# A fused diffusion step: VectorE's chain of Hyena's long convolution cut into finer steps between weight splits

## The chip, the cores and the metric

The kernel runs on one core of one Trainium2 chip. The metric is the device time of one execution in microseconds (us); a lower time is better. Before the change the median of three runs is 1741.65 us (1736.06 to 1744.64).

## The reference

The kernel computes one inference step of a two-layer backbone for 128 context tokens and 512 latent tokens (T = 640 together) with a model width of 1024. Layer 0 mixes by attention on one half of the channels and by Hyena, a long convolution, on the other half; layer 1 is a bidirectional mLSTM; each layer ends with a gated ConvFFN. Around each sub-layer stand an RMS norm and a shift, scale and gate worked out from the conditioning vector (`mod` below). What the change touches is Hyena in layer 0:

```python
def hyena_mixer(u, conv_w, conv_b, w1, b1, w2, b2, w3, b3, sin_freq, skip):
    L = u.shape[1]
    uc = dwconv3(u, conv_w, conv_b)
    x0, x1, v = uc[..., :HY_CH], uc[..., HY_CH:2 * HY_CH], uc[..., 2 * HY_CH:]
    v = (v * x1).astype(jnp.float32)
    h_f, h_b = hyena_filters(L, w1, b1, w2, b2, w3, b3, sin_freq)
    y = long_conv(v, h_f) + jnp.flip(long_conv(jnp.flip(v, axis=1), h_b), axis=1) + skip * v
    return (y * x0).astype(u.dtype)
...
out = jnp.concatenate([attn, hyo], axis=-1) @ w_out
```

`long_conv` is a convolution over the whole sequence by a Fourier transform; `u` is the Hyena part of the input projection `x @ w_in`, and `attn` is softmax attention with a norm and a rotary position (rope) on q and k.

## The kernel before, in words

**Matmuls.** Inputs are float32. A weight tile `wr` (128x1024, loaded by DMA through SyncE, SP) is split into two parts: ScalarE (ACT) casts `wh <- wr`, VectorE (DVE) subtracts `wl <- wr, wh`. TensorE (PE) then makes three products for each pair of tiles: `wh` with the high part of the activation, `wl` with the high part, `wh` with the low part. So no weight tile can be used by PE before ACT's cast and, behind it, DVE's subtraction. In the trace all engine calls stand at line 284 (a helper that records them), matmuls at line 365, transposes at line 376.

**Stages around the change.** The columns of the input projection of Hyena come in twelve tiles, named `u` in the trace, 48 matmuls each. When a tile is done, a width-3 convolution makes `zh` from it: one ACT instruction, then four on DVE. The eight tiles of x1 and v come first, then q, k and v (`qkv`), then the last four tiles, x0, whose `zh` is multiplied into the result of the long convolution by GpSimd (POOL), `vx<-zh,vx`. While PE works at `qkv` and at these last four tiles, DVE and ACT have the long convolution to do, in two halves of 256 channels (`long_conv`, lines 1312 on). Each half has transforms by matmul, sums of them (`forward`, lines 1112 on), products with the filter's spectrum for two groups, g0 and g1 (four products, two sums and four butterflies of halves each), four last sums (`vx`, `vz`), and inverse transforms by matmul (`iy`, `iz`). In the same stretch q and k of token tiles 0 to 4 are normed: ACT squares them, a chain of eleven small DVE instructions makes one over the root (`qn0` to `qn4`), ACT scales by it, DVE multiplies by the gains (`qkg`), POOL or DVE makes the rope products (`qrt`, `qru`), DVE adds them, PE transposes (`qkt`) and ACT copies the result (`qkT`). Then come attention (scores `s`, maximum `mx`, exponential `p`, transposes `pt`, result `po`), the output projection of layer 0 (`o`) in four groups of tokens, and the FFN. The gate that the output projection needs, mod(0,2), is summed on DVE from weights loaded by DMA: two `acc <- mw` instructions for each `mw` tile (`mw` has two buffers), at the end cast (`moda`), split (`modb`) and spread over the partitions by matmul (`modp`).

**What sets the order.** The program is written into each engine's queue in an order that a planner chooses while the kernel is built (class `Order`, lines 60 to 249). The matmuls are the main line. Everything else is a side task, a Python generator. A plain `yield` lets the task go on only when the results it has issued are planned to be done; `yield 0` lets it go on as soon as the planner's PE clock allows. At each call of `pump` (line 191) the planner first looks whether DVE and ACT are planned to be free within `FIRST` = 2500 ns of its clock. If they are, the next weight tile is split; only then do side tasks get a turn. Splits can so stand only between steps of a side task, never within one. The long convolution runs as one side task for both halves with a lead of `HLEAD` = 5000 ns, and has these places where a step can end:

```python
            nc.vector.tensor_tensor(o, x, y, op=op)
            if FINE and n % FINE == FINE - 1:
                yield 0
```

```python
            if FINE:
                yield 0
            nc.vector.tensor_tensor(x[0], x[0], x[1], op=ALU.subtract)
            nc.vector.tensor_tensor(C, C, S, op=ALU.add)
            if FINE:
                yield 0
```

With `FINE = 0` the eight sums of `forward` are one step, and so are the ten instructions of g0 and the ten of g1.

Of the kernel before, what the change touches and what calls it, by code (L numbers as in the profile page):

```python
# [325 lines left out]
def hybrid_step(ctx: ExitStack, tc: tile.TileContext, A: dict, O: dict):  # L326
# [785 lines left out]
    def forward(src, cols, out, name):  # L1112
# [24 lines left out]
        for n, (o, x, y, op) in enumerate(((out[0][:, a], c[:, a], c[:, b], ALU.add), (out[0][:, b], c[:, a], c[:, b], ALU.subtract),  # L1137
# [5 lines left out]
            nc.vector.tensor_tensor(o, x, y, op=op)  # L1143
            if FINE and n % FINE == FINE - 1:
                yield 0
        yield

    FINE = 0

    def filters():  # L1150
        z, w = hy["z"], hy["w"]
# [160 lines left out]
    def long_conv(hf):  # L1312
# [17 lines left out]
        HYE.tensor_tensor(vp[:, h1], vp[:, h1], gr, op=ALU.mult)  # L1330
        if FINE:
            yield 0
# [8 lines left out]
        for n in range(2):  # L1341
# [4 lines left out]
            HYE.tensor_tensor(S, S, gc, op=ALU.mult)  # L1346
# [6 lines that stand above are left out]
# [951 lines left out]
```

## Time and profile before

| | us |
|---|---|
| median of 3 runs (lowest, highest) | 1741.65 (1736.06, 1744.64) |
| the profiled execution, its own time | 1739.15 |
| its span, first to last instruction | 1737.3 |
| TensorE (PE) busy | 1683.4, 97% of the span |
| VectorE (DVE) busy | 1243.6, 72% |
| ScalarE (ACT) busy | 746.3, 43% |
| GpSimd (POOL) busy | 353.8, 20% |
| mean granted TensorE clock | 0.987 of full |

The span is that of the profiled execution; 1.85 us of its time lie around it. An engine's busy time is the time in which an instruction of it ran, waits not counted. A number in square brackets behind an instruction in the rows below is the time for which the engine had stood idle before it, with what ended the wait. A row "x4" of the timeline joins four instructions of one form in a row; its time is from the first one's start to the last one's end. The stretch of interest, from the last part of `qkv` to the start of the FFN of layer 0, lies between 229 and 385 us.

### The profile page before, as it was taken

To read this page: it belongs to the slowest core of one execution; us is meant where nothing else is said; L and a number is where in the kernel's file an instruction comes from. 1 tells how busy PE (TensorE), PEld (TensorE's weight loads), DVE (VectorE), ACT (ScalarE), POOL (GpSimd) and SP (SyncE) were. 2 spreads that over 40 slices of the span, in tenths; PEclk is the share of its full clock that TensorE was granted. 3 is DMA by queue.
4 is the path that set the end of the run, shared out by engine and by line. 5 is a ranking of instruction groups with operands and counts; after the bars stand their busy time and mean duration, and the time that the engine had idled before them with its cause. 6 is when DMAs were issued, how large, how long until landed. Compare 5 with 4: busy or idle time off the path is not lost. (4 is left out here: it accounts for less than half of the span.)

```text
span 1737.3 us, 25489 instructions
## 1 busy us (share of the span) xinstructions
PE 1683.4 (97%) x10074; PEld 1523.0 (88%) x10074; DVE 1243.6 (72%) x2057; ACT 746.3 (43%) x1233; POOL 353.8 (20%) x187
## 2 busy tenths in 40 slices
PE   7899899999999999999999999997999999999997
PEld 2778787789999999888899999996899999998886
DVE  4788797878878888797766888886578744445365
ACT  3422545545434344455565344334354423333343
POOL 0000121001546454340013111120015411111000
PEclk9999999999999999999999999998999999999999
DMA  9245132412434434454523212122124322223343
GB/s 359 91 152 170 37 101 101 169 38 99 158 121 143 144 119 154 153 198 129 188 89 137 70 47 83 57 69 100 49 77 147 125 77 74 73 74 109 132 159 122
DMA packets 64352, 203.85 MB, mean 117 GB/s; under 512 B 7335, under 2 KB 12455, under 8 KB 64234
## 3 DMA queue, kind: packets, MB, share of 16 engines
q1 hardware_dynamic: 64234, 202.23, 33.9%
q8 instruction: 79, 1.29, 0.3%
q14 instruction: 39, 0.32, 0.1%
HBM read 196.17 MB, written 3.94 MB: 115 GB/s over the span
## 5 line engine op out<-in xcount | busy, mean ns | idle before, releaser
L284 DVE TENSOR_TENSOR wl<-wr,wh 128x1024 fp32r<-128x1024 f32 (+1 forms) x260 | 317.9, 1228 | 107.8 <-ACT wh L284 107.6
L284 ACT CAST wh<-wr 128x1024 fp32r<-128x1024 f32 (+1 forms) x260 | 263.5, 1018 | 146.7 <-PE dn L365 104.1
L284 POOL TENSOR_TENSOR hid<-zg,zu 128x640 f32<-128x640 f32 x44 | 105.5, 2398 | 318.5 <-DVE zu L284 305.9
L284 DVE SCALAR_TENSOR_TENSOR acc<-mw,sc,acc 128x1024 f32<-128x1024 f32 x91 | 168.3, 1868 | 2.7 <-DMA mw<-in_w_mod 2.4
L284 POOL TENSOR_TENSOR acc<-acc,modp 128x1024 f32<-128x1024 f32 x49 | 146.2, 2984 | 115.4 <-ACT modp L284 91.2
L284 DVE SCALAR_TENSOR_TENSOR zg<-g,vec,zg 128x127 f32<-128x127 f32 (+3 forms) x168 | 87.4, 541 | 89.4 <-ACT zg L284 86.4
L365 PE MATMUL dn<-wh,hh 128*128 128x512 f32 x440 | 139.1, 396 | 1.8 <-DVE zu L284 1.6
L365 PE MATMUL dn<-wl,hh 128*128 128x512 f32 x440 | 138.2, 394 | 0.0
L365 PE MATMUL dn<-wh,hl 128*128 128x512 f32 x440 | 138.1, 394 | 0.0
L284 DVE SCALAR_TENSOR_TENSOR zu<-u,vec,zu 128x511 f32<-128x511 f32 (+2 forms) x164 | 86.7, 549 | 62.8 <-ACT zu L284 59.9
L284 ACT ACTIVATE zu<-u,vec 128x640 f32<-128x640 f32 (+1 forms) x42 | 36.8, 876 | 173.8 <-PE u L365 173.8
L365 PE MATMUL u<-a3h,wh 128*128 128x384 f32 (+1 forms) x336 | 104.7, 312 | 0.8 <-DVE a3h L284 0.8
L365 PE MATMUL g<-a3h,wh 128*128 128x384 f32 (+1 forms) x336 | 104.8, 312 | 0.0
L365 PE MATMUL g<-a1h,wh 128*128 128x384 f32 (+1 forms) x336 | 104.8, 312 | 0.0
L365 PE MATMUL u<-a3l,wh 128*128 128x384 f32 (+1 forms) x336 | 104.1, 310 | 0.5 <-POOL a3l L284 0.5
L365 PE MATMUL u<-a3h,wl 128*128 128x384 f32 (+1 forms) x336 | 104.3, 310 | 0.2 <-DVE wl L284 0.2
L365 PE MATMUL u<-a1h,wl 128*128 128x384 f32 (+1 forms) x336 | 104.2, 310 | 0.2 <-DVE wl L284 0.2
L365 PE MATMUL u<-a1h,wh 128*128 128x384 f32 (+1 forms) x336 | 104.2, 310 | 0.0
L365 PE MATMUL g<-a3h,wl 128*128 128x384 f32 (+1 forms) x336 | 104.1, 310 | 0.0
L365 PE MATMUL g<-a3l,wh 128*128 128x384 f32 (+1 forms) x336 | 104.1, 310 | 0.0
L365 PE MATMUL g<-a1h,wl 128*128 128x384 f32 (+1 forms) x336 | 104.0, 310 | 0.0
L365 PE MATMUL u<-a1l,wh 128*128 128x384 f32 (+1 forms) x336 | 104.0, 310 | 0.0
(742 smaller groups left out, 4452.2 us busy)
## 6 DMA issues: line engine op xcount, KB each, us to landing
wr<-in_w_up SPq DMA_DIRECT2D x92, 512.0 KB, 3.3
wr<-in_w_down SPq DMA_DIRECT2D x82, 512.0 KB, 3.3
mw<-in_w_mod SPq DMA_DIRECT2D x80, 512.0 KB, 4.4
wr<-in_w_ml SPq DMA_DIRECT2D x34, 512.0 KB, 3.6
wr<-in_w_out SPq DMA_DIRECT2D x18, 512.0 KB, 4.2
wr<-in_w_in SPq DMA_DIRECT2D x13, 512.0 KB
wr<-in_w_u SPq DMA_DIRECT2D x12, 512.0 KB, 5.2
we<-in_w_mod SPq DMA_DIRECT2D x8, 512.0 KB, 7.3
```

The source lines that it names most:

```text
L284: r = f(*args, **kw)
L365: r = nc.tensor.matmul(out, lhsT, rhs, start=start, stop=stop)
```

## The change

One number is changed, from 0 to 2:

```diff
@@ -1145,7 +1145,7 @@
                 yield 0
         yield
 
-    FINE = 0
+    FINE = 2
 
     def filters():
```

Now `forward` may be left after every second of its eight sums, and `long_conv` after the first four products, after the four products of g0 and of g1, and after the two sums behind each of these. No instruction is added or removed. What moves is the order in which the planner writes them: in the first half of the channels nothing but buffer numbers changes, in the second half and behind it, up to the start of the FFN of layer 0, the order changes on every engine; after that only one pair of `modp` matmuls in layer 1 stands one group of matmuls later.

VectorE, second half of the channels, from the end of `forward`: `vx` and `vf` are the tiles of the long convolution, `qsq` the q and k of token tile 2, `wl` a weight split, `qn3v` the first of the eleven of `qn3`.

```order
+L284 TENSOR_TENSOR vx_1773<-vf_1595,g0c 128x512
+L284 TENSOR_TENSOR vx_1774<-vf_1596,g0s 128x512
+L284 TENSOR_TENSOR vf_1595<-vf_1595,g0s 128x512
+L284 TENSOR_TENSOR vf_1596<-vf_1596,g0c 128x512
 L284 TENSOR_TENSOR qsq_1533<-qsq_1533,qrt_1691 128x6x64
 L284 TENSOR_TENSOR qsq_1533<-qsq_1533,qru_1692 128x6x64
-L284 TENSOR_TENSOR wl_1799<-wr_1699,wh_1798 128x1024
-L284 TENSOR_TENSOR wl_1811<-wr_1730,wh_1810 128x1024
-L284 TENSOR_SCALAR qn3v<-qss_1790 128x6
+L284 TENSOR_TENSOR vx_1773<-vx_1773,vx_1774 128x512
+L284 TENSOR_TENSOR vf_1595<-vf_1595,vf_1596 128x512
+L284 TENSOR_TENSOR wl_1811<-wr_1699,wh_1810 128x1024
```

The products and sums of g0 now stand ahead of the split and of `qn3`; one weight split (second of the last four `u` tiles) stands there instead of two (second and third). The third one's split moves behind `qn3` and a `zh`.

ScalarE around the cast of the fourth of these `u` tiles' weights, `wr_1757`. Before:

```order
L284 ACTIVATE qj_1952,qss_1951<-qsq_1816 128x128 x6
L284 ACTIVATE zh_2001<-u_1919,vec 128x640
L284 CAST wh_2014<-wr_1757 128x1024
L284 ACTIVATE zh_2064<-u_2007,vec 128x640
L284 ACTIVATE qsq_1816<-qsq_1816,qn4y 128x128 x6
```

With the change:

```order
L284 ACTIVATE qj_1945,qss_1944<-qsq_1833 128x128 x6
L284 COPY qkT_1126<-qkt_1974 128x128
L284 COPY qkT_1127<-qkt_1974 128x128
L284 COPY qkT_1128<-qkt_1974 128x128
L284 ACTIVATE zh_1992<-u_1913,vec 128x640
L284 ACTIVATE qsq_1833<-qsq_1833,qn4y 128x128 x6
L284 CAST wh_2026<-wr_1757 128x1024
L284 ACTIVATE zh_2078<-u_1998,vec 128x640
```

The cast of `wr_1757` has moved behind the scaling of token tile 4, which needs the last result of the eleven DVE instructions of `qn4`; the DVE split of that tile stands right behind `qn4` too. On POOL the rope products of token tile 3 now stand ahead of the first `vx<-zh,vx`, where they stood behind it. The four last sums `vx`, `vz` stand behind the `zh` of the fourth `u` tile on DVE, and the second half's inverse transforms, with the transposes of token tiles 3 and 4, have moved on PE from within the fourth `u` tile into the start of attention.

VectorE at the end of the splits of the output projection: `o0l` is the low part of its activations, `acc_2205` and `acc_2206` (before: 2309 and 2310) are the two sums of mod(0,2). Before:

```order
L284 TENSOR_TENSOR o0l_2915<-mx_2555,o0h_2914 128x640
L284 SCALAR_TENSOR_TENSOR acc_2309<-mw_2770,sc,acc_2309 128x1024
L284 SCALAR_TENSOR_TENSOR acc_2310<-mw_2770,sc,acc_2310 128x1024
L284 SCALAR_TENSOR_TENSOR acc_2309<-mw_2932,sc,acc_2309 128x1024
L284 SCALAR_TENSOR_TENSOR acc_2310<-mw_2932,sc,acc_2310 128x1024
L284 SCALAR_TENSOR_TENSOR acc_2309<-mw_2948,sc,acc_2309 128x1024
L284 SCALAR_TENSOR_TENSOR acc_2310<-mw_2948,sc,acc_2310 128x1024
L284 TENSOR_TENSOR modb_2993<-acc_2309,moda_2992 128x1024
```

With the change:

```order
L284 TENSOR_TENSOR o0l_2903<-mx_2555,o0h_2902 128x640
L284 SCALAR_TENSOR_TENSOR acc_2205<-mw_2736,sc,acc_2205 128x1024
L284 SCALAR_TENSOR_TENSOR acc_2206<-mw_2736,sc,acc_2206 128x1024
L284 SCALAR_TENSOR_TENSOR acc_2205<-mw_2766,sc,acc_2205 128x1024
L284 SCALAR_TENSOR_TENSOR acc_2206<-mw_2766,sc,acc_2206 128x1024
L284 SCALAR_TENSOR_TENSOR acc_2205<-mw_2940,sc,acc_2205 128x1024
L284 SCALAR_TENSOR_TENSOR acc_2206<-mw_2940,sc,acc_2206 128x1024
L284 SCALAR_TENSOR_TENSOR acc_2205<-mw_2956,sc,acc_2205 128x1024
L284 SCALAR_TENSOR_TENSOR acc_2206<-mw_2956,sc,acc_2206 128x1024
L284 SCALAR_TENSOR_TENSOR acc_2205<-mw_2966,sc,acc_2205 128x1024
L284 SCALAR_TENSOR_TENSOR acc_2206<-mw_2966,sc,acc_2206 128x1024
L284 TENSOR_TENSOR modb_2999<-acc_2205,moda_2998 128x1024
```

Ten of these sums stand between the last split and `modb` where six stood; four of them have left attention. On SP three loads of `mw` instead of two follow the loads of the FFN's first weights there, and on PE all four pairs of `modp` matmuls stand between the last groups of matmuls ahead of the fourth `o` tile.

## Rows read from the trace of the kernel before

**Rows 1.** Windows: us, busy us of each engine (instructions), granted clock, DMA share, GB/s

```profile
251.00:254.00 3.00, 0.07 (x1) 0.00 (x0) 2.93 (x5) 0.88 (x1) 0.82 (x1) 1.00 0.00 0
254.00:258.00 4.00, 3.78 (x13) 3.78 (x14) 3.96 (x6) 0.00 (x0) 1.57 (x1) 0.57 0.38 131
...
265.60:324.00 58.40, 52.72 (x359) 42.46 (x358) 44.50 (x100) 35.70 (x94) 5.58 (x4) 1.00 0.28 102
...
sum 156.00, PE 146.07 PEld 123.20 DVE 126.76 ACT 81.17 POOL 15.20; mean PE 20.87 PEld 17.60 DVE 18.11 ACT 11.60 POOL 2.17
```

**Rows 2.** Timeline of PE: start us, us, operation; in brackets the idle time ahead

```profile
243.69 0.33 PE L365 MATMUL u<-a0h,wh 128*128 128x384 f32 x1
...
250.73 0.34 PE L365 MATMUL u<-a0h,wh 128*128 128x384 f32 x1
254.22 0.69 PE L365 MATMUL u<-a0h,wl 128*128 128x384 f32 x1 [3.15 <-DVE wl L284]
...
269.70 1.02 PE L365 MATMUL s<-qkT,qkT 128*128 128x512 f32 x2
...
270.78 0.61 PE L365 MATMUL iy<-dfi,vx 128*128 128x128 f32 x4
...
360.46 0.70 PE L365 MATMUL o<-wh,o0h 128*128 128x512 f32 x2 [0.60 <-DVE o0p0t L284]
```

**Rows 3.** Timeline of DVE, 228 to 274 us

```profile
228.72 0.54 DVE L284 TENSOR_TENSOR qsq<-qsq,qrt 128x384 f32<-128x384 f32 x1
...
233.16 0.16 DVE L284 TENSOR_SCALAR qn3v<-qss 128x6 f32<-128x6 f32 x1
...
234.99 0.68 DVE L284 TENSOR_TENSOR vx<-vf,g0c 128x512 f32<-128x512 f32 x1
...
239.95 2.17 DVE L284 SCALAR_TENSOR_TENSOR zh<-u,vec,zh 128x511 f32<-128x511 f32 x4
...
242.90 2.06 DVE L284 TENSOR_TENSOR vx<-vf,g1c 128x512 f32<-128x512 f32 x1
...
252.95 1.22 DVE L284 TENSOR_TENSOR wl<-wr,wh 128x1024 fp32r<-128x1024 f32 x1
...
269.11 0.82 DVE L284 TENSOR_REDUCE mx<-s 128x1 f32<-128x640 f32 x1
...
272.61 0.55 DVE L284 TENSOR_SCALAR p<-p,rr 128x640 f32<-128x640 f32 x1
```

**Rows 4.** Timeline of ACT, 228 to 274 us

```profile
235.11 1.87 ACT L284 ACTIVATE qsq<-qsq,qn3y 128x128 f32<-128x128 f32 x6 [2.35 <-DVE qn3y L284]
...
237.35 0.89 ACT L284 ACTIVATE zh<-u,vec 128x640 f32<-128x640 f32 x1
...
245.24 1.03 ACT L284 CAST wh<-wr 128x1024 fp32r<-128x1024 f32 x1
```

**Rows 5.** Timelines of POOL and DVE around 208 us, then POOL later

```profile
208.01 1.90 POOL L284 TENSOR_TENSOR qrt<-qsq,rope 128x384 f32<-128x384 f32 x1 [10.27 <-DVE qsq L284]
...
208.92 1.02 DVE L284 TENSOR_SCALAR qn2v<-qss 128x6 f32<-128x6 f32 x1
...
269.33 1.54 POOL L284 TENSOR_TENSOR vx<-zh,vx 128x640 f32<-128x640 f32 x1 [13.76 <-issue]
```

**Rows 6.** Timelines of POOL and DVE around 450 us

```profile
450.15 3.38 POOL L284 TENSOR_TENSOR acc<-acc,modp 128x1024 f32<-128x1024 f32 x1
...
452.09 2.17 DVE L284 SCALAR_TENSOR_TENSOR zg<-g,vec,zg 128x511 f32<-128x511 f32 x4 [0.83 <-ACT zg L284]
```

**Rows 7.** Timelines of DVE and SP, 340 to 350 us

```profile
340.72 2.48 DVE L284 SCALAR_TENSOR_TENSOR acc<-mw,sc,acc 128x1024 f32<-128x1024 f32 x2
344.75 4.87 DVE L284 SCALAR_TENSOR_TENSOR acc<-mw,sc,acc 128x1024 f32<-128x1024 f32 x4 [1.56 <-DMA mw<-in_w_mod]
...
340.47 3.08 SPq L284 DMA_DIRECT2D mw<-in_w_mod  x2
```

## The prediction

> **What bounds the kernel now.** I start from the busy times in the table above: TensorE works in 97% of the span, no other engine in more than 72%, so the time falls only where PE stops waiting, and grows where it waits longer. Next come the windows of the stretch in which the order changes, 229 to 385 us [rows 1]. The reader should see that PE is busy 146.07 of 156.00 us there, so it idles 9.93 us: 2.93 of it between 251 and 254, 0.22 to 258, and 5.68 during the start of attention and attention (265.6 to 324); 0.60 stands ahead of the fourth `o` tile [rows 2]. In 254 to 258 the granted clock is 0.57, so that 4.00 us do the work of 2.28: another 1.7 us. All that this change can win, by whatever order, is 9.9 + 1.7 = 11.6 us. A measurement of this kernel can tell about 0.5% from no change, 8.7 us, so only almost the whole of it would count as faster.
>
> The timeline of PE then shows what the largest wait is [rows 2]: the fourth of the last `u` tiles starts at 250.73, has one matmul, and stands 3.15 us for `wl`, its weight split. The timeline of DVE shows that split at 252.95 [rows 3], behind the work of Hyena's second half: between 242.90 and 250.87 the products and sums of g1 run as one step. ACT's cast had been done since 246.3 [rows 4]. So here DVE is late, and finer steps could let the split in sooner. Whether they do is read from the new order.
>
> **The change, part by part.** Nothing is added or removed; I rebuild the queues of DVE, ACT and POOL in the new order with the durations of the old trace. A `u` tile takes 7.04 us of PE (243.69 to 250.73, 48 matmuls) [rows 2].
>
> *Third `u` tile.* On DVE g0 now starts at 228.72, where the two rope sums stood [rows 3]. Behind it come: ten instructions of g0, 4.96 us (234.99 to 239.95 before); two rope sums, 1.0; one split, 1.2; eleven of `qn3`, 1.83 (233.16 to 234.99) [rows 3]: `qn3` ends at 237.7, 2.7 us later than before. ACT waits for it with the scaling; from that to the end of its next `zh` took 3.25 us (234.99 to 238.24) [rows 3, 4], so DVE's `zh` starts at about 241.0. DVE has nothing else in its queue and stands about 3.3 us. `zh` takes 2.1, ends at 243.1 and the third tile's split at 244.2. PE wants it at 243.7: a new wait of **0.4 us**.
>
> *Fourth `u` tile.* This is the point that decides. PE reaches it at 251.1. DVE goes on with the four products of g1, 2.4 us at 0.6 each like those of g0; they took longer before, the first 2.06 us [rows 3], because POOL worked beside them, and now POOL's rope products stand behind them. Then the gains of `qkg` 0.9, `zh` 2.1: 249.5. Now the whole `qn4` chain, 1.83 alone. But from 247.5 POOL does two rope products and then two `vx<-zh,vx`, and these meet `qn4`. What that does is shown at 208.92: an instruction of 128x6, 0.16 us otherwise, took 1.02 and ended when POOL's product did (208.01 + 1.90 = 209.91) [rows 3, 5]. A `vx` of POOL takes 1.54 us alone [rows 5]; two in a row, less the DVE work that passes between, are 2.8 us of holding (bounds 0 and 3.1). `qn4` ends at about 254.1. Only then can ACT scale (1.87), cast the fourth tile's weights (1.03) [rows 4] and DVE split them (1.22) [rows 3]: 258.2. PE does one matmul and stands **7.0 us** where it stood 3.15. The slower clock behind the stop I count the same as before, 1.7 us; twice that is the upper bound of it. By the place of the cast alone, the split cannot be on time: even with no holding it comes at 255.4, 4.3 us late.
>
> The Trainium skill ("SBUF — State Buffer", section "Who interferes with whom") says that a DVE instruction with at most one SBUF input outside the two-port modes does not contend with GpSimd, while one with two SBUF inputs is locked out for the whole of a GpSimd instruction that reads SBUF. By that rule `zh`, whose large input comes from PSUM, passes beside the rope products and only the two `vx` count; were `zh` held too, the sum would be about 2 us more. The trace agrees: four `zg` of the same form took 2.17 us beside a POOL instruction that ran from 450.15 to 453.53 [rows 6], as long as `zh` without POOL [rows 3].
>
> *Start of attention.* The fourth tile ends at about 266.6. ACT's and DVE's `zh` take 3.0, the four last sums of the convolution, now behind them, 2.4, and from the first maximum to the first scaled `p` it takes 4.05 (269.11 to 273.16) [rows 3]: 9.5 us until PE gets its first `p`. PE has the moved work to fill them: four groups of transposes at 0.33, three pairs of scores at 1.08 (269.70 to 270.78) and one `iy`, four groups at 0.45, 1.8 [rows 2]: 6.4. It idles **3.1 us** (bounds 1.0 and 4.6). In the rest of attention four `acc` instructions of 1.22 us [rows 7] have left DVE. PE idled 5.68 in this window [rows 1], 0.6 of it at the start; I let two thirds of the 4.9 us come back to PE and keep **1.8** (bounds 0 and 5.1).
>
> *Output projection.* Those four `acc` come due behind the last split. Counted from the first `o` matmul, S: before, S is 324.0, the splits end at 340.7 and the fourth `o` tile starts at 360.46, S + 36.45, with 0.60 of waiting [rows 2, 7]. Now no `acc` stands ahead of the splits, so they end at about S + 16.0, and four `acc` at S + 20.8. The third `mw` can be asked for only when the first buffer is read, S + 18.5, and the fifth when the third has been read. From the first issue to the use before lay 4.3 us (340.47 to 344.75); the two issues are drawn over 3.08, so for one load I take 3.4 to 4.2 [rows 7]. Two such loads in a chain, with the `acc` between them, put the end of the sums at S + 29.3 to S + 30.6. From there to the fourth `o` tile (`moda`, `modb`, four pairs of `modp`, the matmul groups between them, `o0p0t`) it took 10.8 before (349.62 to 360.46) [rows 2, 7]; with the first `modp` closer behind, 10.6. The tile starts at S + 39.9 to S + 41.2, 3.4 to 4.7 later: I take **3.9**. The norm and the FFN behind it shift as a whole, and PE had no idle time there to take it up.
>
> *Sum.* PE's idle time: 0.4 + 7.0 + 3.1 + 1.8 + (0.7 + 3.9) = 16.9 for 9.9 before, **+7.0 us**. The profiled execution took 1739.15 (its span 1737.3), so 1746.2; the median of the runs lies 2.5 above that execution, 1741.65, so I say **1748.6**.
>
> **Rivals.** *The wait shrinks all the same.* POOL starts so that it passes between and holds nothing (minus 2.8), attention's rest idles 0 (minus 1.8), the loads of `mw` land in 3.4 (minus 0.5): +1.9, 1743.5. For it: the order in which two engines meet is a matter of tenths of a us. Against: POOL's four products are 6.0 us of work that becomes ready at 247.4, and `qn4` falls in the middle. I give the stretch from 0 to +3 a chance of 0.15.
>
> *Slower by over 0.5%.* The mechanism is the chain of mod(0,2) with its two buffers, on top of the late split. Attention absorbs none of what left it (+3.3, to 5.1), because its waits come from ACT (`p`, `pt`), not from DVE. The loads take 4.2 us (+0.8) and a second stretch of slow clock follows the stop at the start of attention (+1.5): +12.6, 1754.2. It decides where attention's idle time stays above 4 us and the chain of loads exceeds S + 30. For it: DVE is busy in only 44.50 of 58.40 us of attention [rows 1], so it may not have been what was short. Chance 0.30.
>
> *The split is in time.* The fourth tile's comes by 251, attention starts without a stop, and nothing is late behind it: up to minus 10, 1731.6. Against it stands the cast behind `qn4` on ACT, which no duration of the trace brings ahead of 251. Chance 0.04.
>
> *Nothing happens*, since the steps allow other places but the planner takes none: true of the first half of the channels, false of the second, where the cast, the splits and the `acc` move. It is part of the same-speed cases.
>
> **How the numbers follow.** Forecast, +3 to +8.7: 0.51; rival one 0.15; slower 0.30; faster 0.04. Within 0.5%: 0.66, slower 0.30, faster 0.04. The range reaches from just below rival one to past the sum of the upper bounds, 1739.5 to 1756.0, with about 2 us for the scatter of a median.
>
> **What would show it.** In the profile after: the third tile's `wl` ends at about 244; DVE stands some 3 us ahead of `zh` near 238; two of the `qn4` instructions take over 1 us; the cast follows ACT's scaling by `qn4y`, and PE's stop ahead of the fourth `u` tile is 6 to 7.5 us. Attention's window idles less than 5.7 us, and the stop ahead of the fourth `o` tile grows to 4 or 5. The prediction is wrong if the stop at the fourth tile is below 4 us, if attention idles as before, or if the time goes below 1739.

## The result, and the profile after

Six runs of the changed kernel have a median of 1752.59 us (1747.87 to 1755.05), six of the kernel before beside them 1741.01. The ratio is 1.0070, with a 95% interval of 1.0047 to 1.0093: slower by 0.7%, 12 us, a small change, but the interval leaves out 1. That lies in the range of the forecast (1739.5 to 1756.0) and beyond its likeliest case. The profiled execution of the changed kernel took 1747.87, the lowest of the six, with a span of 1746.1; it stands 8.7 above the profiled execution of before. One run of e8 below, of 2374.65 us, is a slow one and is left out of all means and ratios.

The two executions differ ahead of the change too (the first of the last four `u` tiles starts at 226.07 us, before at 228.94, with the same order up to there; 1.45 of these 2.87 us are idle time of PE), so I count from that start. The first `u` tile to the first matmul of the FFN takes 168.98 us now and took 156.17: **+12.8**. Windows of this stretch in the changed kernel, same columns as [rows 1]:

```profile
248.50:253.99 5.49, 0.00 (x0) 0.00 (x0) 2.42 (x10) 2.84 (x8) 1.24 (x1) 0.70 0.00 0
...
256.00:258.00 2.00, 2.00 (x8) 2.00 (x8) 2.00 (x4) 0.00 (x0) 0.00 (x0) 0.50 0.80 260
258.00:260.00 2.00, 2.00 (x8) 2.00 (x7) 1.93 (x5) 0.00 (x0) 0.00 (x0) 0.50 0.01 2
260.00:262.00 2.00, 2.00 (x11) 2.00 (x10) 2.00 (x6) 0.00 (x0) 0.00 (x0) 0.76 0.26 78
...
265.00:268.07 3.07, 1.67 (x12) 1.00 (x10) 2.02 (x4) 2.87 (x13) 0.00 (x0) 1.00 1.00 407
268.07:274.67 6.60, 5.30 (x28) 3.70 (x29) 5.13 (x12) 3.06 (x6) 0.00 (x0) 1.00 0.53 217
...
313.00:328.43 15.43, 12.47 (x85) 10.57 (x84) 9.05 (x21) 8.79 (x25) 0.00 (x0) 0.92 0.19 69
328.43:368.65 40.22, 36.01 (x155) 28.38 (x154) 32.31 (x36) 18.89 (x29) 0.00 (x0) 1.00 0.46 157
368.65:395.05 26.40, 25.30 (x120) 20.36 (x121) 21.00 (x47) 13.06 (x21) 4.05 (x4) 1.00 0.17 61
sum 168.98, PE 150.06 PEld 126.28 DVE 128.66 ACT 83.41 POOL 15.22; mean PE 8.34 PEld 7.02 DVE 7.15 ACT 4.63 POOL 0.85
```

PE is idle for 168.98 - 150.06 = 18.9 us where it was idle for 9.9 [rows 1]: **+9.0**. And the slow stretch has grown. The same view for single pieces, two of the kernel before and then four of the changed one:

```profile
228.94:385.11 156.17, 146.24 (x844) 123.37 (x843) 126.82 (x245) 81.34 (x187) 15.31 (x11) 0.99 0.28 97
254.22:257.40 3.18, 3.18 (x10) 3.18 (x11) 3.14 (x4) 0.00 (x0) 1.35 (x1) 0.50 0.48 165
...
251.00:253.99 2.99, 0.00 (x0) 0.00 (x0) 0.13 (x2) 2.84 (x8) 0.00 (x0) 0.50 0.00 0
253.99:260.90 6.91, 6.33 (x19) 5.94 (x20) 6.84 (x13) 0.74 (x1) 0.00 (x0) 0.50 0.23 76
274.67:313.00 38.33, 36.64 (x254) 30.47 (x255) 29.48 (x67) 21.86 (x54) 6.17 (x4) 0.99 0.05 15
312.20:315.50 3.30, 3.30 (x14) 2.82 (x14) 0.55 (x1) 1.13 (x3) 0.00 (x0) 0.50 0.03 5
```

Before, PE works for 3.2 us at 0.50 of full clock (1.2 of 2.4 GHz), which costs 1.6. Now it works for 6.3 us at that clock behind the stop (3.2 lost) and for another 3.4 in attention (1.7 lost): **+3.3**. With the idle time that is 12.3 of the 12.8. In the changed kernel the clock has also fallen before the stop is over, while PE had nothing to do. The stops, in the timeline of PE of the changed kernel:

```profile
253.99 0.69 PE L365 MATMUL u<-a0h,wh 128*128 128x384 f32 x1 [5.50 <-ACT wh L284]
255.25 0.69 PE L365 MATMUL u<-a0h,wl 128*128 128x384 f32 x1 [0.57 <-DVE wl L284]
...
274.67 0.73 PE L376 MATMUL pt<-ident,p 128*128 128x128 f32 x5 [1.30 <-DVE p L284]
...
323.68 1.38 PE L365 MATMUL po<-pt,vv 128*128 128x128 f32 x10 [2.23 <-ACT pt L284]
...
358.98 0.50 PE L365 MATMUL modp<-moda,onesr 128*128 128x512 f32 x1 [1.12 <-ACT moda L284]
360.43 0.50 PE L365 MATMUL modp<-modb,onesr 128*128 128x512 f32 x1 [0.95 <-DVE modb L284]
368.65 0.69 PE L365 MATMUL o<-wh,o0h 128*128 128x512 f32 x2 [2.14 <-DVE o0p0t L284]
...
384.61 0.55 PE L376 MATMUL o0p0nt<-ident,o0p0t 128*128 128x128 f32 x3 [1.10 <-DVE o0p0ny L284]
```

The first two answer to the wait of 3.15 in [rows 2], the last but one to the 0.60 there. The timelines of POOL (the first three lines) and DVE behind it:

```profile
244.75 1.02 POOL L284 TENSOR_TENSOR qrt<-qsq,rope 128x384 f32<-128x384 f32 x1 [24.66 <-DVE qsq L284]
245.72 1.02 POOL L284 TENSOR_TENSOR qru<-qsq,rope 128x384 f32<-128x384 f32 x1
246.69 3.05 POOL L284 TENSOR_TENSOR vx<-zh,vx 128x640 f32<-128x640 f32 x2
...
237.99 2.18 DVE L284 SCALAR_TENSOR_TENSOR zh<-u,vec,zh 128x511 f32<-128x511 f32 x4 [3.19 <-ACT zh L284]
...
244.50 2.17 DVE L284 SCALAR_TENSOR_TENSOR zh<-u,vec,zh 128x511 f32<-128x511 f32 x4
246.58 0.18 DVE L284 TENSOR_SCALAR qn4v<-qss 128x6 f32<-128x6 f32 x1
246.80 1.48 DVE L284 TENSOR_SCALAR qn4y<-qn4v 128x6 int32<-128x6 int32 x1
248.31 1.45 DVE L284 SCALAR_TENSOR_TENSOR qn4q<-qn4v,qn4y 128x6 f32<-128x6 f32 x1
...
253.97 1.22 DVE L284 TENSOR_TENSOR wl<-wr,wh 128x1024 fp32r<-128x1024 f32 x1 [2.86 <-ACT wh L284]
...
265.98 2.18 DVE L284 SCALAR_TENSOR_TENSOR zh<-u,vec,zh 128x511 f32<-128x511 f32 x4 [3.41 <-ACT zh L284]
```

DVE waits 3.19, 2.86 and 3.41 us for ACT ahead of attention, 9.5 together; before, 1.14 and 1.52. Behind the third wait stands PE, not ACT's own work: ACT itself had stood for 10.34 us until the fourth `u` tile was done. `zh` at 244.50 runs beside POOL's rope products at its usual 2.17; the two `qn4` instructions beside POOL's `vx` take 1.48 and 1.45 instead of 0.17. And at the end of the output projection the ten sums of mod(0,2), in DVE's timeline, waiting for their loads three times:

```profile
343.91 4.86 DVE L284 SCALAR_TENSOR_TENSOR acc<-mw,sc,acc 128x1024 f32<-128x1024 f32 x4
350.21 2.48 DVE L284 SCALAR_TENSOR_TENSOR acc<-mw,sc,acc 128x1024 f32<-128x1024 f32 x2 [1.44 <-DMA mw<-in_w_mod]
352.91 2.48 DVE L284 SCALAR_TENSOR_TENSOR acc<-mw,sc,acc 128x1024 f32<-128x1024 f32 x2 [0.22 <-DMA mw<-in_w_mod]
356.56 2.48 DVE L284 SCALAR_TENSOR_TENSOR acc<-mw,sc,acc 128x1024 f32<-128x1024 f32 x2 [1.17 <-DMA mw<-in_w_mod]
```

**Waits and clock apart.** Each run lists its time and its mean granted clock. The product of the two (time at full clock) and what is left of the time (lost clock) separate, roughly, what the clock does from the rest; 0.001 of clock is 1.7 us, so I use means over all runs. For the kernel before they are 1717.0 and 21.0, 1717.0 and 21.9, 1717.1 and 20.6 us in the three sets of runs of the experiments. For the changed kernel they are **1724.1 and 28.0**. So 7.1 us of the loss are there at full clock. How much is clock is less sure. The difference is 6 to 7 against these sets; the six runs of before that were taken beside the changed kernel have no clock on record, but their mean of 1740.4 us, less 1717.0, would leave 23.4 lost and a difference of 4.6 (an estimate). And lost clock, so counted, holds half of any stop in which the clock is already low: in the profiled stretch 6.8 us, of which 1.9 lie in the stop itself. Waits and slow matmuls are told apart there by the trace alone, +9.0 and +3.3.

### The profile page after: what moved, and what is told of

Read it like the earlier page. It is cut to its first block, busy times and chain, and to the rows that moved or that the text cites. A ratio compares the mean times of both kernels' runs of the same rounds, so it can differ in the third digit from the quotient of the medians.

```text
span 1746.1 us, 25487 instructions
## 1 busy us (share of the span) xinstructions
PE 1684.2 (96%) x10074; PEld 1523.4 (87%) x10074; DVE 1242.6 (71%) x2057; ACT 745.9 (43%) x1233; POOL 352.7 (20%) x187
## 5 line engine op out<-in xcount | busy, mean ns | idle before, releaser
L284 DVE TENSOR_TENSOR wl<-wr,wh 128x1024 fp32r<-128x1024 f32 (+1 forms) x260 | 321.6, 1241 | 114.4 <-ACT wh L284 114.1
L365 PE MATMUL u<-a3h,wh 128*128 128x384 f32 (+1 forms) x336 | 104.3, 310 | 0.8 <-DVE a3h L284 0.8
L365 PE MATMUL g<-a1l,wh 128*128 128x384 f32 (+1 forms) x336 | 104.7, 311 | 0.0
L365 PE MATMUL g<-a1h,wl 128*128 128x384 f32 (+1 forms) x336 | 104.3, 311 | 0.0
```

Of the source, the lines that this page charges most:

```text
L284: r = f(*args, **kw)
L365: r = nc.tensor.matmul(out, lhsT, rhs, start=start, stop=stop)
```

## The experiments

Theory A at the start: two separate costs, the late split of the fourth `u` tile (with its slow clock) and the late sums of mod(0,2). Rivals: B, the sums alone; C, the finer steps lengthen the work of DVE wherever the split stands. In the second set, D: what is gained at one stop is lost at the next. In the third, E and F, as their expectations say. The table gives, in us, the profiled execution's stretch from the first of the last `u` tiles to the first `o` matmul (**ahead**), from there to the FFN (**behind**), and over the runs the ratio to before with its interval, the mean time at full clock and the mean lost clock. Ahead and behind are of one execution each and hold its slow clock; the last two columns are means.

| run | ahead | behind | ratio | full clock | lost |
|---|---|---|---|---|---|
| before | 95.1 | 61.1 | | 1717.0 | 21.0 |
| changed | 102.4 | 66.6 | 1.0070 (1.0047 to 1.0093) | 1724.1 | 28.0 |
| e1 no last step | 102.7 | 70.0 | 1.0090 (1.0069 to 1.0111) | 1724.5 | 28.9 |
| e2 forward only | 105.8 | 62.1 | 1.0070 (1.0049 to 1.0090) | 1725.3 | 24.5 |
| e3 fine, split early | 106.5 | 62.0 | 1.0070 (1.0049 to 1.0091) | 1724.8 | 25.1 |
| e4 coarse, split early | 102.1 | 61.5 | 1.0050 (1.0032 to 1.0068) | 1721.9 | 24.7 |
| e5 fine, no `vx` | 99.5 | 70.2 | 1.0057 (1.0037 to 1.0078) | 1722.2 | 26.2 |
| e6 fine, no late sums | 102.4 | 64.2 | 1.0035 (1.0020 to 1.0049) | 1719.7 | 25.4 |
| e7 coarse, late sums | 97.9 | 75.1 | 1.0088 (1.0065 to 1.0111) | 1725.3 | 28.1 |
| e8 coarse, no `vx` | 93.0 | 62.6 | 0.9992 (0.9978 to 1.0006) | 1714.7 | 22.4 |
| e9 fine, early sums | 104.3 | 60.2 | 1.0060 (1.0039 to 1.0082) | 1721.3 | 27.4 |
| e10 coarse, early sums | 97.5 | 60.2 | 1.0013 (0.9999 to 1.0028) | 1717.6 | 22.5 |
| e11 fine, neither | 99.4 | 64.2 | 1.0020 (1.0007 to 1.0032) | 1717.6 | 23.8 |
| e12 coarse, late `vx`, early sums | 96.2 | 60.2 | 0.9989 (0.9975 to 1.0002) | 1714.1 | 21.7 |

### e1 to e4: the split in time

e1, the step behind the eighth sum of `forward` taken away. That step is followed by the plain `yield` with nothing between, so the wait for results of the sums is lost with it:

```diff
-            if FINE and n % FINE == FINE - 1:
+            if FINE and n % FINE == FINE - 1 and n < 7:
```

Expected: 

> Steps as in the change, except that forward has none behind its eighth sum, so that its plain yield waits for the sums again. The fourth u tile's cast and split then stand ahead of qn4, right behind zh of the second tile; ten acc still stand behind the last split of the output projection. Theory A (the late split and the late sums of mod(0,2) are two separate costs): the stop ahead of the fourth u tile falls from 6.9 us to 0 to 2, the slow clock behind it with it, and the stop ahead of the fourth o tile stays at some 4 us: 1741 - 4 + 4 + up to 3 in attention, so 1741 to 1745. Theory B (all of the loss is the chain of mod(0,2), a late split would be taken up by attention): as the change, 1751 to 1754. Theory C (the finer steps themselves make the DVE stretch longer, wherever the split stands): the stop moves to the start of attention, 1750 or more.

e2, steps in `forward` alone (the three in `long_conv` are taken out). Expected: 

> Steps in forward alone, none in long_conv. The fourth split stands where it stood before (behind zh of the second tile, ahead of qn4) but behind g1 as one step; six acc stand behind the last split, as before. Theory A: neither cost is there, a stop of 2 to 4 us ahead of the fourth u tile as before, and about 1 at the fourth o tile: 1739 to 1744. Theory B: the same, 1741. Theory C: slower, 1746 or more, since DVE's work is cut as in the change.

e3 and e4, the same edit in the changed kernel and in the kernel before:

```diff
         for n in range(2):
+            if hf and n:
+                od.idle()
```

Expected of e3: 

> The change with one thing more: ahead of g1 of the second half the planner is told to split the next weight tile at once. The fourth tile's split then stands right behind the third's; six acc stand behind the last split. Theory A: no stop ahead of the fourth u tile and no slow clock (minus 4.7 us against before), no late sums of mod(0,2): 1736 to 1739 if attention stays as it was, 1741 if its start waits for the work that was moved back. Theory B: 1741, as before. Theory C: 1746 or more.

Expected of e4: 

> The kernel before, with the split of the fourth u tile told to stand ahead of g1, and no finer steps. Six acc behind the last split. Theory A: as e3, 1736 to 1739, since the split is what counts and not the size of the steps. Theory B: 1741. Theory C: 1736 to 1739, and clearly faster than e3.

Measured: 1753.52, 1749.97, 1749.99 and 1745.16 us, beside 1738.29. None is where A put it. The split did come earlier: in e4 PE has no wait at all in the four `u` tiles and ends them 28.7 us after the first one's start; before the change it was 36.5, with the wait and the inverse transforms within. But then it stands, in the timelines of PE of e4 (three lines), e1, e2 and e3:

```profile
260.31 1.54 PE L376 MATMUL qkt<-ident,qsq 128*128 128x128 f32 x6 [3.46 <-DVE qsq L284]
262.84 2.08 PE L365 MATMUL s<-qkT,qkT 128*128 128x512 f32 x2 [0.99 <-ACT qkT L284]
...
292.79 0.77 PE L376 MATMUL pt<-ident,p 128*128 128x128 f32 x5 [2.42 <-ACT p L284]
...
261.61 1.51 PE L376 MATMUL qkt<-ident,qsq 128*128 128x128 f32 x6 [5.39 <-DVE qsq L284]
...
272.37 0.87 PE L376 MATMUL qkt<-ident,qsq 128*128 128x128 f32 x3 [9.23 <-DVE qsq L284]
...
265.91 1.51 PE L376 MATMUL qkt<-ident,qsq 128*128 128x128 f32 x6 [9.43 <-DVE qsq L284]
```

In e1 the first stop there is 5.39, in e2 9.23 and in e3 9.43 us, each for `qsq` from DVE and each with 2 to 4 us lost to the slow clock behind it (e2 keeps a stop of 1.89 at the fourth tile too). So the late split is the place where PE waits, not by itself the cost: ahead of attention PE waits for what DVE and ACT have still to do (q and k of the last token tiles), at the fourth tile or behind it. As I read the kernel before, PE's wait of 3.15 us left the inverse transforms and the transposes ready to fill the fourth tile. Theory A falls as far as the split goes. B falls too: e2 to e4 have six sums behind the last split, as before, and are slower all the same. C as I put it falls with e4, which has no finer steps and is slower; the other half of C, that e4 would be clearly faster than e3, came true (4.8 us).

### e5 to e8: one cost taken away, the order kept

For e5, e6, e8 and e11 the planner books an instruction as always but it is not issued, so every other one keeps its place:

```diff
-            r = f(*args, **kw)
+            r = None if self.od.mute else f(*args, **kw)
...
+        od.mute = i < 2
         nc.gpsimd.tensor_tensor(vx[i][:, 0:T], z[:, 0:T], vx[i][:, 0:T], op=ALU.mult)
+        od.mute = False
```

The second piece is that of e5 and e8; in e6 the same is done around the loads and `acc` of tiles 6 and 7 of mod(0,2). e7 has `SLACK1 = 1250.0`. Expected:

e5: 

> The change in exactly its order, less two POOL instructions: the products of Hyena's output for the first two of four channel tiles (vx<-zh,vx) are left out, so those two keep the convolution's result without the gate. Theory A (POOL's two products hold qn4, and that chain is on the path): the two held instructions fall from 1.48 and 1.45 to 0.17, the fourth split comes 2.6 us sooner, the stop ahead of the fourth u tile falls from 6.3 to 3.6, and u1 to the first o matmul from 102.4 to 99 or 100: 1747.5 to 1750.5. Theory D (what is gained at one stop is lost at the next, since attention starts when DVE and ACT are through, wherever PE stood): the stop shrinks as in A, but u1 to the first o matmul stays at 101.5 to 102.5, 1751 to 1754.

e6: 

> The change in exactly its order, less the last two of eight weight tiles of mod(0,2): their two loads and four acc instructions are left out, so that gate is summed over 768 of 1024 inputs. Six acc stand behind the last split then, as before the change. Theory A (the late sums with two buffers are a cost of their own): the waits ahead of modp and of the fourth o tile fall from 5.3 us together to about 1, first o matmul to start of the FFN from 66.6 to 62 or 63: 1747.5 to 1750. Theory D: the stop ahead of the fourth o tile is set by something else (o0p0t, the exponents' table), at most 1 us is gained: 1751 to 1753.

e7: 

> The kernel before, with the planner's slack for mod(0,2) cut from 1500 to 1250 ns: the order up to attention is the same, but five acc leave attention and twelve instead of six stand behind the last split of the output projection. Theory A, as my forecast had it: the first o matmul to the FFN grows from 61.1 by 5 to 8 us, and attention gives back two thirds of 6 us of DVE, idling 1 to 2 instead of 5.1: 1740 to 1744 in all. Rival A2 (attention's waits are not DVE's lack of time): attention still idles 4.5 to 5.5, and the whole of the late sums counts: 1744 to 1749.

e8: 

> The kernel before in exactly its order, less the same two POOL products. Theory A: the first product of g1 falls from 2.06 to 0.7, the split of the fourth u tile comes 1.4 us sooner, its stop falls from 3.15 to 1.8; the two rope products on DVE behind it fall from 2.37 to 1.0, and attention starts 2.5 us sooner: 1736 to 1739. Theory D: the time is as before, 1739 to 1742, since PE stops longer at the next place.

Measured: 1749.23, 1744.12, 1752.27 and 1737.18 us, beside 1738.21.

e5: without the hold the fourth tile's stop falls to 2.92 + 0.57, and the stretch ahead from 102.4 to 99.5, as A said and not D. In e5's profiled execution (1752.04 us) the output projection then waits longer for the same sums. In its timeline of PE:

```profile
253.70 0.69 PE L366 MATMUL u<-a0h,wh 128*128 128x384 f32 x1 [2.92 <-ACT wh L285]
...
360.29 0.50 PE L366 MATMUL modp<-moda,onesr 128*128 128x512 f32 x1 [2.97 <-ACT moda L285]
...
371.52 0.71 PE L366 MATMUL o<-wh,o0h 128*128 128x512 f32 x2 [2.14 <-DVE o0p0t L285]
```

and 3.4 us are lost to the slow clock there, half behind the stops at `modp` and half behind that at the fourth `o` tile. That looks like D, but the runs do not bear it out: at full clock their mean is 1.9 us below the changed kernel's, as much as the same omission gives where the late sums are away (e11 below).

e6: with six sums behind the last split the waits ahead of `modp` are gone, 2.14 at the fourth `o` tile stays, and the time is 4.4 us less at full clock and 2.6 less in lost clock than the changed kernel's, more than A said. This is the larger part of the 7.1 us, and it is shown. The profiled execution of e6 took 1750.54 us, well above the median, with 1.7 us lost to the slow clock at the fourth `o` tile.

e7: the kernel before with twelve sums late is as slow as the changed kernel, though its order ahead of attention is that of before. Behind the first `o` matmul it takes 14 us more than before, 8.2 of them idle time and 5.1 slow clock. And attention, which five `acc` have left, idles 6.9 us instead of 5.1. Two lines of e7's PE timeline:

```profile
319.37 1.17 PE L376 MATMUL pt<-ident,p 128*128 128x128 f32 x6 [2.03 <-DVE p L284]
...
360.88 0.80 PE L365 MATMUL modp<-moda,onesr 128*128 128x512 f32 x1 [4.63 <-ACT moda L284]
```

So A2: attention gives nothing back. The time lies 3 us above A2's range all the same, since the late sums cost more than the 5 to 8 us that both theories had for them.

e8: the same hold costs the kernel before 2.1 us ahead. In the profiled execution 1.5 of it is lost again at the sums; at full clock the runs have 2.3 less than before, but the ratio is not told apart from 1.

### e9 to e12: the sums early, and both costs away

e9 and e10 have `SLACK1 = 2500.0`, in the changed kernel and in the one before; e11 joins e5 and e6; e12 is e10 with the first two `vx` products left out of their places, as in e5, and issued behind the third:

```diff
+        if i < 2:
+            later.append((vx[i][:, 0:T], z[:, 0:T]))
+        elif later:
+            for v, y in later:
+                tc.nc.gpsimd.tensor_tensor(v, y, v, op=ALU.mult)
+            later.clear()
```

Expected:

e9: 

> The change, with the planner's slack for mod(0,2) raised from 1500 to 2500 ns: the order up to attention is that of the change, but eleven of the fourteen acc stand in attention and one instead of ten behind the last split of the output projection. Theory E (the late sums are the larger part of the loss, the rest is the u tiles and the start of attention): first o matmul to FFN falls from 66.6 to 61 or 62, u1 to the first o matmul stays at 101 to 104 even with more acc in attention: 1744 to 1747. Rival F (acc costs the same wherever it stands, since DVE is short of time in attention too): attention takes 5 to 10 us longer, 1749 to 1754.

e10: 

> The kernel before, with the same slack of 2500 ns: two acc instead of six behind the last split, nine instead of six in attention. Theory E: in the kernel before the sums are done just in time, so almost nothing is gained: 1736 to 1740 beside 1738 to 1741 for the kernel before. Rival F: attention takes 3 to 4 us longer, 1741 to 1744.

e11: 

> The change in exactly its order, less both things that were left out singly: the two POOL products of Hyena's output, and the last two of eight weight tiles of mod(0,2). Theory E: with the sums out of the way, what is gained ahead of attention is kept to the end: 2.8 us less than e6, 1740 to 1742. Rival D (a gain ahead is lost at the next stop, whatever that is): as e6, 1743 to 1746.

e12: 

> The kernel before with two edits: the two POOL products are issued behind the third one, in attention, where they hold no chain (nothing is left out), and the slack for mod(0,2) is 2500 ns. Theory E: 2 us gained ahead of attention, kept since the sums come early: 1735 to 1738 beside 1738 to 1741, at the edge of what can be told. Rival D: as the kernel before.

Measured: 1748.66, 1740.31, 1741.51 and 1735.31 us, beside 1737.46.

e9: behind the first `o` matmul the stretch falls from 66.6 to 60.2, as E said, and the stretch ahead grows by 1.9. At full clock that is 2.8 less than the changed kernel; the clock lost is almost the same. Moving the sums gains less than leaving them out did in e6 (4.4). The ratio can't be told from that of the changed kernel: a miss by 2 us, E only in part. e10: the part behind falls to 60.2 here too, but attention, with three more `acc`, idles 7.1 us instead of 5.1, and the time is not told apart from before.

e11: 1717.6 at full clock, 2.0 less than e6: the gain ahead is kept, E and not D. As e5 keeps as much (1.9) with the late sums in place, it is kept there too; D falls, and with it E's condition that the sums be out of the way. The kernel to compare it with is e8, which lacks the same `vx`, has all its sums and has 1714.7: of the 7.1 us, 2.9 are left with the sums away, and the profiled executions show them ahead of the `o` tiles (99.4 and 93.0, of which 3 is slow clock). Two pairs of kernels that differ in `FINE` alone leave about as much: e3 and e4 2.9, e9 and e10 3.7 at full clock. So some 3 us belong to the finer steps wherever the split and the sums stand; by what mechanism is not shown.

e12, which leaves nothing out, has the lowest median, but its interval takes in 1: a version that may beat both kernels by 0.1%, not shown to.

## Why the prediction was right or wrong

The sign and the range held; the likeliest case, within 0.5%, did not come, but the slower one, to which I gave 0.30. One of the signs that I had named for being wrong came true: attention idles about as before (4.6 us behind its start, before 5.1).

- **Right, the third and fourth `u` tile.** DVE stood 3.19 us (forecast 3.3), the third split cost 0.19 (0.4). Counted from the first tile's start, `qn4` ended at 25.1 us (25.2) and the fourth split at 29.1 (29.3). The hold by POOL was 2.6 us (2.8) in two instructions of over 1 us, at the place named; by e5 it is worth 2.8 ahead of the `o` tiles. By e8 the kernel before pays 2.1 for its own holds, so they are hardly any part of the difference. PE's stop was 6.07 (7.0). The Trainium skill ("SBUF — State Buffer", section "Who interferes with whom") has a DVE instruction contend with GpSimd when two of its inputs lie in SBUF, and with one such input only in a two-port mode. The trace agrees for `zh`, which passed beside POOL at 2.17 us, and for `qn4q`, which has two and took 1.45 instead of 0.17. But `qn4y` has one and was held as long (1.48); whether it ran in a two-port mode no run here shows.
- **Right, the start of attention**: 2.7 us of idle time there, forecast 3.1.
- **Right, the sums of mod(0,2).** The fourth `o` tile starts 40.22 us after the first `o` matmul; forecast 39.9 to 41.2. The hit is in part luck. By its own durations the forecast's chain of loads ends at S + 30.1 to S + 31.7, not S + 29.3 to S + 30.6. It ended at S + 30.6, the two loads of the chain having taken 3.8 and 3.9, and from there to the tile it took 9.6 us where I had 10.6.
- **Wrong, "I let two thirds of the 4.9 us come back to PE and keep 1.8".** Attention idles 4.6 us, before 5.1. e7, with five fewer `acc`, idles more than before (6.9), and e10, with three more, does too (7.1). So the amount of DVE's work does not decide it. The waits there are for `p` and `pt` through DVE and ACT in turn; that their order decides is my reading, not shown. This step mis-sized the sum by 2.8.
- **Wrong, "The slower clock behind the stop I count the same as before, 1.7 us".** In the profiled stretch PE's slow matmuls cost 3.2 behind the fourth tile and another 1.7 in attention, 3.3 more than before; over the runs lost clock, counted with the stops, is some 5 to 7 more. With idle time at +9.0 instead of +7.0 this is what lies between the forecast and the +12.8 of the stretch.
- **Wrong, small: no loss behind the fourth `o` tile.** That part takes 26.40 us, before 24.65: 1.10 of it is the wait of transposes for `o0p0ny`.

The rival that ends slower had three conditions. Two came true, attention that absorbs next to nothing and more slow clock. Of its third, the loads took less than its 4.2 us, but their chain did end behind S + 30. That the forecast of waits, +7.0, stands beside 7.1 at full clock is luck: in the profiled stretch idle time grew by 9.0, and the 7.1 count only half of the time that a stop lasts at the low clock. Term by term (forecast in brackets) the idle time is 0.2 (0.4), 6.1 (7.0), 2.7 (3.1), 4.6 (1.8), 4.2 (4.6) and 1.1 (0).

What the runs did not settle: why e2, e3 and e4 lose 7 to 11 us ahead of the `o` tiles though their sums come as before. In e2 and e3 the first transposes of `p` come about 10 us later than before, counted from the first `u` tile; in e4 they come 1 us sooner, and attention idles 8.0 us instead of 5.1. Each wait is seen, its cause in the order was not taken apart. Nor was that of the 3 us that the finer steps leave.

## What to carry to other kernels

When a chain on one engine is cut finer so that something urgent may go between, look at what covered that engine's trips to another one: here the products had covered ACT's scaling, and without them DVE stood twice for 3 us. A stop of the main engine that you see is where the lateness shows; four kernels that removed or shortened it had a stop of 3 to 9 us further on, so count to the next point where everything has to be there. And price a stop with the clock behind it, as a range.

## What the runs showed of the hardware

The clock cost about a third of what the waits did in the profiled stretch (+3.3 beside +9.0 us). After the stop of 3.15 us ahead of the fourth tile, matmuls of 384 columns took 0.52 us instead of 0.34 (the lower level, 1.2 GHz) until 257.3, for 3 us; after the stop of 5.50 and 0.57, until 260.9, 5.6 us. But the length of the stop does not give the length of the slow stretch. At the same place e7 has the same stop of 3.15 us, and PE works at the lower level for 6 us behind it; e8 has a stop of 1.77, and a slow stretch of 3.4 us begins 1 us behind its end; e2 has one of 1.89 and none. The windows of e7 and e8:

```profile
251.37:257.40 6.03, 6.03 (x19) 6.03 (x20) 5.68 (x17) 0.00 (x0) 1.36 (x1) 0.50 0.26 87
252.30:255.70 3.40, 3.40 (x13) 3.40 (x12) 3.12 (x13) 0.00 (x0) 0.00 (x0) 0.50 0.43 149
```

In e5 a stop of 2.97 ahead of `modp` was followed by 3.4 us at the lower level (1.7 lost), in the changed kernel's profiled execution a stop of 1.12 at the same instruction by none. The stop of 2.14 at the fourth `o` tile was followed by such a stretch in e5 and e6 and by none in the changed kernel. Runs of one program differ largely by this: of the changed kernel's six, those of 1747.87 us at a mean clock of 0.987 and of 1755.05 at 0.983 have the same 1725 at full clock (all six: 1722 to 1725).
